# A decoder trunk on one core: the experts' sum starts at zero, and each expert's rows bring half of the residual

## The chip, the cores and the metric

One core of a Trainium2 chip. The metric is device time in microseconds (us) of one execution. The engines are TensorE (PE; PEld is its weight load), VectorE (DVE), ScalarE (ACT), GpSimd (POOL) and SyncE (SP). Each has its own queue and takes its instructions in order; they meet through semaphores. Transfers are started from SP, ACT or POOL.

## The reference, cut to what matters

Two layers. Each is attention (three kinds of heads and one output projection), a sum with the scaled input and a layer norm, then a mixture of experts and a second layer norm. Each of the 512 tokens goes to one group of four, and to two of the eight experts in that group:

```
for l in range(DEPTH):                                   # 2
    mix = hybrid_mixer(x, ...)
    x = layer_norm(ALPHA * x + mix, ln1_g[l], ln1_b[l])
    moe = hier_moe(x, ...)      # top-1 group, top-2 experts, 32 experts of width 256
    x = layer_norm(ALPHA * x + moe, ln2_g[l], ln2_b[l])
```

So the second norm's input is, up to the factor ALPHA, the row x of the token plus two expert rows. x is a normalized row times the gain ln1_g plus the bias ln1_b.

## The kernel before

Everything is float32, with 1024 columns. Tokens lie in four tiles `yn[0..3]` of 128 rows. After the output projection each tile is normalized on ACT (L919), without gain and bias, and its rows are written to DRAM as `xd` from ACT's queue (L920). DVE works out the router's logits `Lg` (L917), the group maximum `gm` (L932), the chosen experts' mask `selb` (L960), the position of each token in its expert's list `posm` (L972), and one-hot matrices `oneh` (L1054). With these and a token table (`tok`) PE makes the lists: for each slot of an expert the index of its row (`ri`) and its weight (`rv`). An expert has 64 slots, and two experts make a pair of 128 rows.

`first_rows(i)` (L885 to L890) belongs to this stage: two DVE operations of 128x1024 multiply tile i by the gain and add the bias (both broadcast in `gb1`, loaded once a layer), and ACT's queue writes the result to the DRAM tensor `y2`. It is called for tiles 0 to 2 in the loop over tiles and for tile 3 after the first gathers. DVE's order mixes these operations into the routing. `y2` is the sum to which the experts' rows are added.

The expert stage runs over 16 pairs p, in these steps:

- gather (L1000, POOL): 128 rows of `xd` into one of two x slots of the tile `xroom`;
- turned (L1011 on PE, L1015 on ACT, L1017 on DVE): transposes, with gain and bias on the way out of PSUM, into `xg`;
- experts_up (L97, tile S): gate and up matmuls of both experts; experts_mid: silu on ACT (L1031) and the product `h` on DVE (L1032);
- experts_down: transposes of h (L297) copied to `hT`, then the matmuls into the two PSUM banks `o`; their evacuation, times the weight `rv`, by ACT (L1044, first 512 columns) and DVE (L1045, second 512) into one of three y slots of `xroom`, which take turns (`row_room`);
- scatter (L1046, POOL): an indirect transfer that adds the 128 rows to `y2`.

PE works in the order S(p), hT(p), o(p), S(p+1), with the transposes of later pairs in between. The weights, 6 MB a pair, come over SP's queue (L530) in units of 1.5 MB into a ring of 13 units; a unit is loaded again when its last reader is done. The x slots, the y slots and one of these units share `xroom`, and fill it. After the 16 pairs follow a short loop for experts with more than 64 tokens (overflow, 64 rows at a time), the reading of `y2` (L1251), and the second norm with `gb2`.

Of the kernel before, what the change touches and what calls it, by code (L numbers as in the profile page):

```python
# [64 lines left out]
def trunk(tc, a, out, dbg=None):  # L65
# [4 lines left out]
    with es:  # L70
# [177 lines left out]
        for l in range(DEPTH):  # L248
# [285 lines left out]


            dp = xhp.tile([128, 2 * NK * S], F32, name="dp", tag="xh")
            stC = small.tile([128, 3, NT, 2, 4], F32, name="stC", tag="stC", bufs=1)
# [344 lines left out]
            gb1 = norm_rows(0)  # L882
            y2 = dr.tile([S, D], F32, name="y2", tag="y2")

            def first_rows(i):  # L885

                z = yn[i] if i < NT - 1 else at.tile([128, D], F32, name="x1", tag="u", bufs=3)
                V.tensor_tensor(z, yn[i], gb1[:, 0], OP.mult)
                V.tensor_tensor(z, z, gb1[:, 1], OP.add)
                A.dma_start(y2[128 * i:128 * i + 128, :], z)  # L890

            load_next(2)
# [10 lines left out]
            for i in range(NT):  # L903
                z = yn[i]
                out_proj(i, 2, 768, 1024)
                if i == 0:
                    zt(NT - 1, 0, 3)
                    zt(NT - 1, 3, 6)
                zt(i, 6, 8)
                V.bn_stats(bst[i][:, 1], z[:, 512:1024])  # L910
                t = bank("S")
                for k in range(NK):
                    mm(t[:, :36], zT[i][:, k], rwg[:, k], k == 0, k == NK - 1)
                mv = norm_scale(bst[i], LN_EPS)
                lt = small.tile([128, 36], F32, name="lt", tag="lt")
                V.scalar_tensor_tensor(lt, rsum, mv[:, 0:1], t[:, :36], op0=OP.mult, op1=OP.subtract)
                V.scalar_tensor_tensor(Lg[:, i], lt, mv[:, 3:4], rb, op0=OP.mult, op1=OP.add)  # L917
                V.tensor_tensor(mv[:, 4:5], mv[:, 0:1], mv[:, 3:4], OP.mult)
                A.activation(z, z, AF.Identity, scale=mv[:, 2:3], bias=mv[:, 4:5])  # L919
                A.dma_start(xd[128 * i:128 * i + 128, :], z)  # L920
                if i:
                    first_rows(i - 1)
            xroom = xhp.tile([128, 2 * NK * S], F32, name="xroom", tag="xh")
# [80 lines left out]
            def turned(xr):  # L1004
# [13 lines left out]
                return xg  # L1018

            halves_ = ((0, 64), (64, 128))  # L1020

# [12 lines left out]

            def experts_down(h, w, rows):
                hT = cp.tile([128, 2, 128], F32, name="hT", tag="rw")
                transposes(hT.rearrange("p a b -> p (a b)"), [h[:, 0:128], h[:, 128:256]], 128)
                o = [bank("o") for _ in range(2)]
                for f in range(2):
                    for n in range(2):  # L1040
                        for j, (c0, c1) in enumerate(halves_):
                            last_on["PE"] = mm(o[n][c0:c1], hT[:, f, c0:c1], down(w[j], f, n), f == 0, f == 1)
                y = row_room()
                last_on["A"] = A.activation(y[:, 0:512], o[0], AF.Copy, scale=rows[1])  # L1044
                last_on["V"] = V.tensor_scalar(y[:, 512:1024], o[1], rows[1], None, op0=OP.mult)  # L1045
                return G.indirect_dma_start(out=y2, out_offset=bass.IndirectOffsetOnAxis(ap=rows[0], axis=0), in_=y,  # L1046
                                            in_offset=None, bounds_check=S - 1, oob_is_err=False, compute_op=OP.add)

            RI, XR, XG = {}, {}, {}

# [46 lines left out]
            for p in range(2):  # L1097
                fetch(p)
            first_rows(NT - 1)
            attn.__exit__(None, None, None)  # L1100
            moe = tc.tile_pool(name=f"moe{l}", bufs=1, reuse_waits="tile")
            mo = units["m"] = moe.__enter__()
            load_next(3)
            XG[0] = turned(XR.pop(0))
            lists(1)
# [30 lines left out]
            def overflow():  # L1136

                n_items = nc.values_load(eidi[0:1, MAX_ITEMS:MAX_ITEMS + 1], min_val=0, max_val=MAX_ITEMS)
                with tc.For_i(0, n_items) as item:
# [63 lines left out]
                    for f in range(2):  # L1203
                        for h, c in enumerate(two):
                            mm(o[c], hT[:, f], down(w, f, h), f == 0, f == 1)
                    y = row_room()
                    A.activation(y[0:64, 0:512], o[0:64], AF.Copy, scale=wr[0:64])
                    V.tensor_scalar(y[0:64, 512:1024], o[64:128], wr[64:128], None, op0=OP.mult)
                    G.indirect_dma_start(out=y2, out_offset=bass.IndirectOffsetOnAxis(ap=ri[0:64], axis=0), in_=y[0:64], in_offset=None,
                                         bounds_check=S - 1, oob_is_err=False, compute_op=OP.add)  # L1210

            for p in range(NE // 2):
# [4 lines left out]
                if p + 1 < NE // 2:  # L1217
                    XG[p + 1] = turned(XR.pop(p + 1))
                    fetch(p + 3)
                if p % 2 == 0 and p // 2 + 2 < NE // 4:  # L1220
                    lists(p // 2 + 2)
                st = experts_down(h, w, RI.pop(p))
                load_next()
# [3 lines left out]
                if p == 3:  # L1227
                    pieces()
                    gb2 = norm_rows(1)

            last = l == DEPTH - 1
            with tc.issue_after(last_on["PE"].ins), tc.issue_after(last_on["A"].ins), tc.issue_after(last_on["V"].ins), tc.issue_after(st.ins):
                if not last:
# [11 lines left out]
            for j in range(2):  # L1245
                yu = carve(unit("A", "yt"), 0, [2, D])
                for i in range(2):
# [7 lines left out]
            for i in range(NT):  # L1255
# [6 lines left out]
                for t, c in zip(src, halves):  # L1262
                    V.scalar_tensor_tensor(z[:, c], t, mv[:, 0:1], gb2[:, 0, c], op0=OP.subtract, op1=OP.mult)
                for c in halves if i in (0, 3) else [slice(0, 1024)]:
                    V.scalar_tensor_tensor(z[:, c], z[:, c], mv[:, 2:3], gb2[:, 1, c], op0=OP.mult, op1=OP.add)  # L1265
                if last:
# [76 lines left out]
```

## Time and profile before

| | us |
|---|---|
| median of 3 runs | 1382.35 (1379.83 to 1384.95) |
| the profiled execution | 1385.0 |
| its span in the trace | 1383.2 |
| expert stage, first to last scatter, layer 0 | 434.98 to 660.88 |
| expert stage, first to last scatter, layer 1 | 1108.26 to 1330.18 |

The page is of one execution. Its first part gives each engine's busy time, its second the busy share in 40 slices of 34.6 us, with the granted TensorE clock and the share of the DMA engines. The views of the trace give the instructions of a stretch in order of time, each with the idle time of its engine before it and what ended that, and for transfers the time from issue to landing. A time of a row is from the start of the span.

### The profile page before, as it was taken

The numbers are of one execution on the slowest core, as the hardware profiler recorded it, in microseconds if no ns is written. First come the engines' busy times: TensorE is split into PE (matmuls) and PEld (weight loads), VectorE is DVE, ScalarE is ACT, GpSimd is POOL, SyncE is SP. The second block draws the span as 40 slices with busy tenths as digits, with TensorE's granted clock in tenths as the row PEclk, the third lists the DMA queues.
The fourth block names the chain that finished last, engine by engine and source line by source line (L and its number), as shares of the span: only waits on it lengthen the run. The fifth ranks groups of instructions, "written<-read, shape, count | busy, mean of one in ns | idle before, by whom it ended". The sixth has DMA issues, their size and how long they took to land. (4 is left out here: it accounts for less than half of the span.)

```text
span 1383.2 us, 18273 instructions
## 1 busy us (share of the span) xinstructions
PE 1194.4 (86%) x6701; PEld 815.8 (59%) x6708; DVE 696.6 (50%) x1822; ACT 442.9 (32%) x1050; POOL 292.5 (21%) x286
## 2 busy tenths in 40 slices
PE   6989999999939989887599999999996699898860
PEld 6989976668924533222398899666795343332320
DVE  7599638684552422111668892668636333211125
ACT  3362256673102221111235322857611122111100
POOL 5332431201001121100332334230000122111011
PEclk9999999999969999999799999999998799999985
DMA  7321440115397999998552224200426899999943
GB/s 240 116 80 51 128 158 11 36 40 185 118 402 279 400 413 405 409 390 287 166 165 78 65 83 140 98 23 22 156 104 247 347 384 407 409 403 410 356 166 123
DMA packets 63898, 293.81 MB, mean 212 GB/s; under 512 B 16064, under 2 KB 20672, under 8 KB 48192
## 3 DMA queue, kind: packets, MB, share of 16 engines
q1 hardware_dynamic: 52128, 267.43, 50.5%
q0 software_dynamic: 9376, 16.81, 4.9%
q10 hardware_dynamic: 2304, 8.39, 1.5%
q8 instruction: 54, 0.88, 0.3%
q14 instruction: 36, 0.29, 0.1%
HBM read 278.06 MB, written 31.82 MB: 224 GB/s over the span
## 5 line engine op out<-in xcount | busy, mean ns | idle before, releaser
L97 PE MATMUL acc<-U,xh 128*128 128x384 f32 (+1 forms) x1584 | 298.9, 343 | 18.9 <-DVE xh L212 7.0
L97 PEld LDWEIGHTS acc<-U,xh 128*128 128x128 f32 x1584 | 280.5, 193 | 21.9 <-issue 6.9
L97 PE MATMUL S<-w,xg 128*64 128x512 f32 (+1 forms) x968 | 272.0, 608 | 10.6 <-DMA w<-w_e 8.9
L97 PEld LDWEIGHTS S<-w,xg 128*64 128x64 f32 x968 | 83.1, 141 | 138.8 <-issue 112.9
L1017 DVE TENSOR_SCALAR xg<-acc,lv 128x128 f32<-128x128 f32 x128 | 45.8, 404 | 179.6 <-PE S L97 142.9
L97 PE MATMUL o<-w,hT 128*64 128x512 f32 x488 | 125.4, 603 | 5.9 <-ACT hT L90 3.4
L199 POOL TENSOR_TENSOR U<-raw,U 128x768 fp32r<-128x768 f32 (+2 forms) x46 | 90.3, 1967 | 166.9 <-ACT U L196 166.9
L1046 POOL DMA_INDIRECT y<-xroom,ri x32 | 51.4, 1607 | 294.8 <-DVE xroom L1045 180.5
L1031 ACT ACTIVATE h<-S 128x256 f32<-128x256 f32 x32 | 12.3, 383 | 270.6 <-PE S L97 270.6
L196 ACT ACTIVATE U<-raw 128x768 fp32r<-128x768 f32 (+2 forms) x88 | 68.0, 812 | 71.6 <-PE acc L97 43.7
L1045 DVE TENSOR_SCALAR xroom<-o,rv 128x512 f32<-128x512 f32 x32 | 24.0, 751 | 117.7 <-PE o L97 117.7
L97 PEld LDWEIGHTS o<-w,hT 128*64 128x64 f32 x488 | 39.2, 138 | 67.1 <-issue 57.4
L1000 POOL DMA_INDIRECT xroom<-xd,ri x33 | 35.2, 1066 | 180.5 <-PE acc L1011 94.5
L199 DVE TENSOR_TENSOR U<-raw,U 128x768 fp32r<-128x768 f32 (+2 forms) x42 | 52.8, 1260 | 36.5 <-ACT U L196 34.0
L1011 PEld LDWEIGHTS acc<-cst,xroom 128*128 128x128 f32 x256 | 29.4, 147 | 60.6 <-issue 36.0
L90 ACT ACTIVATE uc<-T 128x512 f32<-128x512 f32 (+3 forms) x117 | 51.3, 460 | 40.9 <-PE T L297 39.1
L1015 ACT ACTIVATE xg<-acc,lv 128x128 f32<-128x128 f32 x128 | 48.9, 458 | 45.5 <-PE T L97 35.8
L1011 PE MATMUL acc<-cst,xroom 128*128 128x128 f32 x256 | 43.7, 298 | 22.7 <-DMA xroom<-xd,ri 20.7
L97 PE MATMUL acc<-U,oh 128*128 128x384 f32 (+1 forms) x384 | 63.3, 315 | 0.0
L1044 ACT ACTIVATE xroom<-o,rv 128x512 f32<-128x512 f32 x32 | 22.0, 687 | 111.0 <-PE o L97 111.0
L97 PEld LDWEIGHTS acc<-U,oh 128*128 128x128 f32 x384 | 56.8, 189 | 1.2 <-issue 1.0
L403 DVE MATCH_REPLACE8 uc<-m,uc 128x256 f32<-128x256 f32 (+2 forms) x96 | 51.4, 539 | 0.0
(367 smaller groups left out, 1942.0 us busy)
## 6 DMA issues: line engine op xcount, KB each, us to landing
w<-w_e SPq DMA_DIRECT2D x110, 1536.0 KB
raw<-w_in SPq DMA_DIRECT2D x64, 384.0 KB
xroom<-w_e SPq DMA_DIRECT2D x8, 1536.0 KB
w<-w_e SPq DMA_DIRECT2D x24, 512.0 KB
raw<-w_o SPq DMA_DIRECT2D x16, 384.0 KB
gb<-ln_rows SPq DMA_DIRECT2D x4, 1024.0 KB
xd<-yn ACTq DMA_DIRECT2D x8, 512.0 KB
y<-yn ACTq DMA_DIRECT2D x6, 512.0 KB
```

Of the source, the lines that this page charges most:

```text
L90: A.activation(o, i, AF.Copy, scale=1.0 if scale is None else scale)
L97: return PE.matmul(o, l, r, start=start, stop=stop, skip_group_check=True)
L196: A.activation(hi, r, AF.Copy)
L199: e.tensor_tensor(lo, r, hi.bitcast(F32), OP.subtract)
L403: V.match_replace(out=acc_t[i][:, :n], in_to_replace=m8, in_values=acc_t[i][:, :n], imm_value=TAKEN)
L1000: G.indirect_dma_start(out=xr[0:n], out_offset=None, in_=xd, in_offset=bass.IndirectOffsetOnAxis(ap=ri[0:n], axis=0), bounds_check=S - 1, ...
L1011: PE.transpose(t[:, 128 * j:128 * j + 128], xr[:, 128 * k:128 * k + 128], ident)
L1015: A.activation(xg[:, k], o, AF.Identity, scale=lv[:, 0, k, 0:1], bias=lv[:, 0, k, 1:2])
L1017: V.tensor_scalar(xg[:, k], o, lv[:, 0, k, 0:1], lv[:, 0, k, 1:2], op0=OP.mult, op1=OP.add)
L1044: last_on["A"] = A.activation(y[:, 0:512], o[0], AF.Copy, scale=rows[1])
L1045: last_on["V"] = V.tensor_scalar(y[:, 512:1024], o[1], rows[1], None, op0=OP.mult)
L1046: return G.indirect_dma_start(out=y2, out_offset=bass.IndirectOffsetOnAxis(ap=rows[0], axis=0), in_=y, in_offset=None, bounds_check=S - 1, ...
```

## The change

- `y2` is made in the attention stage: POOL fills a small tile with zeros and one transfer on SP's queue writes it over all of `y2` (2 MB). `first_rows` is gone, with its eight DVE pairs and its eight transfers.
- `gb1` is multiplied by 0.5 on ACT, once a layer.
- A new function `half_rows` (L1016 to L1021 of the changed kernel) takes the next y slot and writes half of the gathered rows, times gain plus bias, into it: two DVE operations of 128x1024 (L1019, L1020). It is called one pair ahead, beside `turned`. Since each token has two expert rows, the two halves add up to its residual row.
- The two evacuations from PSUM become two DVE operations that add `o` times the weight to the y slot (L1048). ACT has none of it any more. The scatter (now L1049) is as it was. The overflow loop does the same with 64 rows.
- The second norm's gain and bias come in two transfers on SP's queue after the expert weights, into parts of the units that also hold the rows of `y2`.

```diff
@@ attention
+            y2 = dr.tile([S, D], F32, name="y2", tag="y2")
+            none = ring("P")
+            G.memset(none, 0.0)
+            SP.dma_start(y2.rearrange("(p r) c -> p (r c)", r=NT).rearrange("p (n c) -> p n c", c=512), none.unsqueeze(1).to_broadcast([128, 2 * NT, 512]))
@@ out_proj and routing
             gb1 = norm_rows(0)
-            y2 = dr.tile([S, D], F32, name="y2", tag="y2")
-
-            def first_rows(i):
-
-                z = yn[i] if i < NT - 1 else at.tile([128, D], F32, name="x1", tag="u", bufs=3)
-                V.tensor_tensor(z, yn[i], gb1[:, 0], OP.mult)
-                V.tensor_tensor(z, z, gb1[:, 1], OP.add)
-                A.dma_start(y2[128 * i:128 * i + 128, :], z)
-
+            A.activation(gb1.rearrange("p a d -> p (a d)"), gb1.rearrange("p a d -> p (a d)"), AF.Copy, scale=0.5)
...
-                if i:
-                    first_rows(i - 1)
...
+            def half_rows(xr, n=128):
+
+                y = row_room()
+                V.tensor_tensor(y[0:n], xr[0:n], gb1[0:n, 0], OP.mult)
+                V.tensor_tensor(y[0:n], y[0:n], gb1[0:n, 1], OP.add)
+                return y
+
@@ experts_down
-            def experts_down(h, w, rows):
+            def experts_down(h, w, rows, y):
...
-                y = row_room()
-                last_on["A"] = A.activation(y[:, 0:512], o[0], AF.Copy, scale=rows[1])
-                last_on["V"] = V.tensor_scalar(y[:, 512:1024], o[1], rows[1], None, op0=OP.mult)
+                for n in range(2):
+                    c = slice(512 * n, 512 * n + 512)
+                    last_on["V"] = V.scalar_tensor_tensor(y[:, c], o[n], rows[1], y[:, c], op0=OP.mult, op1=OP.add)
@@ the loop over pairs
-                    XG[p + 1] = turned(XR.pop(p + 1))
+                    XG[p + 1], HR[p + 1] = turned(XR[p + 1]), half_rows(XR.pop(p + 1))
                     fetch(p + 3)
...
-                st = experts_down(h, w, RI.pop(p))
+                st = experts_down(h, w, RI.pop(p), HR.pop(p))
...
-                    gb2 = norm_rows(1)
...
+            yus = [unit("A", "yt") for _ in range(2)]
+            gb2 = [yu[:, 2 * D:3 * D] for yu in yus]
+            for j in range(2):
+                SP.dma_start(gb2[j], a["ln_rows"][l:l + 1, 1, j].to_broadcast([128, D]))
```

A scheduler sets the order within each engine, so the order of the program text is not the order of the queues. First DVE's queue in the expert stage of layer 1, around the evacuation of pair 6 (PE_49, Activation_49, DVE_49 and DMASW0 to DMASW7 are semaphores: of engines, and of POOL's indirect transfers, which take the eight in turn). The kernel before, from the copy of hT(6) to the xg of pair 9:

```order
L92 COPY hT<-T 128x256 [waits PE_49]
L1017 TENSOR_SCALAR xg<-acc,lv 128x128
L1045 TENSOR_SCALAR xroom<-o,rv 128x512 [waits PE_49]
L1017 TENSOR_SCALAR xg<-acc,lv 128x128 [waits PE_49]
L1032 TENSOR_TENSOR h<-h,S 128x256 [waits Activation_49]
L1017 TENSOR_SCALAR xg<-acc,lv 128x128 x3
```

The same place in the changed kernel, from the copy of hT(6) to the xg of pair 9:

```order
L92 COPY hT<-T 128x256 [waits PE_49]
L1013 TENSOR_SCALAR xg<-acc,lv 128x128
L1048 SCALAR_TENSOR_TENSOR xroom<-o,rv,xroom 128x512 [waits PE_49] x2
L1019 TENSOR_TENSOR xroom<-xroom,gb 128x1024 [waits DMASW3_49,DMASW0_49,DVE_49]
L1020 TENSOR_TENSOR xroom<-xroom,gb 128x1024 [waits DVE_49]
L1013 TENSOR_SCALAR xg<-acc,lv 128x128 [waits PE_49]
L1035 TENSOR_TENSOR h<-h,S 128x256 [waits Activation_49]
L1013 TENSOR_SCALAR xg<-acc,lv 128x128 x3
```

Between the rows of y(6) and the product h(7) now stand the half rows of pair 9, and the first of them waits for two indirect transfers: the gather of pair 9, whose rows it reads, and the scatter of pair 6, whose slot it takes.

The second place is DVE's queue in the routing of layer 1, from the mask of the chosen experts to the one-hots. The kernel before:

```order
L955 MATCH_REPLACE hot<-top_8922,le 128x8 x3
L888 TENSOR_TENSOR x_9040<-yn,gb 128x1024 [waits Activation_49]
L956 TENSOR_SCALAR hot<-hot 128x32 [waits DVE_49]
L889 TENSOR_TENSOR x_9040<-x_9040,gb 128x1024 [waits DVE_49]
L960 TENSOR_TENSOR selb<-ghot,hot 128x128 [waits DVE_49]
L972 SCALAR_TENSOR_TENSOR posm<-S,selb 128x128 [waits DVE_49,PE_49]
L888 TENSOR_TENSOR yn<-yn,gb 128x1024 [waits DMAHW1_49]
L1054 TENSOR_TENSOR oneh<-posm,cst 128x256 [waits DVE_49]
L889 TENSOR_TENSOR yn<-yn,gb 128x1024 [waits DVE_49]
L1054 TENSOR_TENSOR oneh<-posm,cst 128x256 x3
```

The changed kernel, the same stretch:

```order
L951 MATCH_REPLACE hot<-top_8940,le 128x8 x3
L952 TENSOR_SCALAR hot<-hot 128x32 [waits DVE_49]
L956 TENSOR_TENSOR selb<-ghot,hot 128x128 [waits DVE_49]
L968 SCALAR_TENSOR_TENSOR posm<-S,selb 128x128 [waits DVE_49,PE_49]
L1114 COPY cnt<-S 128x32
L1057 TENSOR_TENSOR oneh<-posm,cst 128x256 [waits DVE_49]
L1057 TENSOR_TENSOR oneh<-posm,cst 128x256 x3
```

The four operations of first_rows are gone from between the mask and the one-hots, and with them the wait for DMAHW1, the write of a tile's rows to `xd`.

## Rows read from the trace of the kernel before

**Rows 1.** The page: busy time of the engines, and the DMA share by slices.

```profile
PE 1194.4 (86%) x6701; PEld 815.8 (59%) x6708; DVE 696.6 (50%) x1822; ACT 442.9 (32%) x1050; POOL 292.5 (21%) x286
...
DMA  7321440115397999998552224200426899999943
```

**Rows 2.** The chain that ended last: start us, us, what; first and last piece.

```profile
1205.24 35.27 DMA w<-w_e
...
1303.25 13.78 DMA w<-w_e
```

**Rows 3.** Stretches: length, busy of PE, PEld, DVE, ACT, POOL, clock, DMA, GB/s.

```profile
1180.00:1240.00 60.00, 53.43 (x244) 19.49 (x242) 14.74 (x50) 10.63 (x26) 10.50 (x8) 1.00 1.02 408
```

**Rows 4.** DVE in time, routing of layer 1: start us, us, instruction, [idle before <-releaser].

```profile
1055.92 0.17 DVE L932 TENSOR_REDUCE gm<-Lg 128x4 f32<-128x16 f32 x1
...
1061.25 0.28 DVE L960 TENSOR_TENSOR selb<-ghot,hot 128x128 bf16<-128x128 f32 x1
1062.14 0.29 DVE L972 SCALAR_TENSOR_TENSOR posm<-S,selb 128x128 f32<-128x128 f32 x1 [0.60 <-PE S L97]
1067.73 1.22 DVE L888 TENSOR_TENSOR yn<-yn,gb 128x1024 f32<-128x1024 f32 x1 [5.30 <-DMA xd<-yn]
...
1070.35 1.09 DVE L1054 TENSOR_TENSOR oneh<-posm,cst 128x256 fp32r<-128x256 f32 x3
```

**Rows 5.** DVE in time, the same place in layer 0.

```profile
382.76 0.17 DVE L932 TENSOR_REDUCE gm<-Lg 128x4 f32<-128x16 f32 x1
387.66 1.23 DVE L888 TENSOR_TENSOR yn<-yn,gb 128x1024 f32<-128x1024 f32 x1 [4.74 <-DMA xd<-yn]
...
395.03 0.29 DVE L960 TENSOR_TENSOR selb<-ghot,hot 128x128 bf16<-128x128 f32 x1
```

**Rows 6.** The chain that ended last: the first gather of layer 1.

```profile
1077.57 10.06 DMA xroom<-xd,ri
```

**Rows 7.** POOL in time: the first and sixteenth scatter of each layer.

```profile
434.98 1.63 POOL L1046 DMA_INDIRECT y<-xroom,ri  x1 [7.17 <-issue]
...
660.88 2.13 POOL L1046 DMA_INDIRECT y<-xroom,ri  x1 [15.48 <-ACT U L196]
...
1108.26 1.62 POOL L1046 DMA_INDIRECT y<-xroom,ri  x1 [7.47 <-issue]
...
1330.18 1.63 POOL L1046 DMA_INDIRECT y<-xroom,ri  x1 [13.68 <-DVE h L1146]
```

**Rows 8.** All engines in time: one pair of layer 1, from xg to the next scatters.

```profile
1295.49 0.41 DVE L1017 TENSOR_SCALAR xg<-acc,lv 128x128 f32<-128x128 f32 x1 [8.08 <-PE S L97]
...
1295.91 0.42 DVE L1032 TENSOR_TENSOR h<-h,S 128x256 f32<-128x256 f32 x1
...
1296.38 0.44 PE L297 MATMUL T<-cst,h 128*128 128x128 f32 x2 [0.94 <-DVE h L1032]
...
1301.00 0.75 DVE L1045 TENSOR_SCALAR xroom<-o,rv 128x512 f32<-128x512 f32 x1 [3.71 <-PE o L97]
...
1302.48 1.56 POOL L1046 DMA_INDIRECT y<-xroom,ri  x1 [12.72 <-issue]
...
1314.94 1.55 POOL L1046 DMA_INDIRECT y<-xroom,ri  x1 [10.90 <-DVE xroom L1045]
```

**Rows 9.** The scatter's line L1046: issue to landing, all 32.

```profile
DMA to landing us min/median/max: 6.8/10.5/12.0
```

**Rows 10.** A stretch after a gap of PE, columns as in rows 3.

```profile
590.00:592.00 2.00, 1.21 (x5) 0.79 (x5) 1.79 (x6) 1.40 (x5) 0.00 (x0) 0.50 1.01 424
```

**Rows 11.** All engines in time, around that stretch.

```profile
586.68 0.64 PE L97 MATMUL S<-xroom,xg 128*64 128x512 f32 x1 [1.95 <-DMA xroom<-w_e]
...
590.61 0.66 PE L297 MATMUL T<-cst,h 128*128 128x128 f32 x2 [1.02 <-DVE h L1032]
...
597.01 0.75 DVE L1045 TENSOR_SCALAR xroom<-o,rv 128x512 f32<-128x512 f32 x1 [4.96 <-PE o L97]
```

**Rows 12.** The scatter's line L1046 again, the one at 1302.48 alone.

```profile
DMA to landing us min/median/max: 9.1/9.1/9.1
```

More of the change, by code (lines that the diff above doesn't have):

```diff
@@ L1042, in experts_down @@
                             last_on["PE"] = mm(o[n][c0:c1], hT[:, f, c0:c1], down(w[j], f, n), f == 0, f == 1)
-                y = row_room()
-                last_on["A"] = A.activation(y[:, 0:512], o[0], AF.Copy, scale=rows[1])
-                last_on["V"] = V.tensor_scalar(y[:, 512:1024], o[1], rows[1], None, op0=OP.mult)
+                for n in range(2):
+                    c = slice(512 * n, 512 * n + 512)
+                    last_on["V"] = V.scalar_tensor_tensor(y[:, c], o[n], rows[1], y[:, c], op0=OP.mult, op1=OP.add)
                 return G.indirect_dma_start(out=y2, out_offset=bass.IndirectOffsetOnAxis(ap=rows[0], axis=0), in_=y,
                                             in_offset=None, bounds_check=S - 1, oob_is_err=False, compute_op=OP.add)
-            RI, XR, XG = {}, {}, {}
+            RI, XR, XG, HR = {}, {}, {}, {}
             def hots(b):
@@ L1098, in trunk @@
                 fetch(p)
-            first_rows(NT - 1)
             attn.__exit__(None, None, None)
@@ L1103, in trunk @@
             load_next(3)
-            XG[0] = turned(XR.pop(0))
+            XG[0], HR[0] = turned(XR[0]), half_rows(XR.pop(0))
             lists(1)
@@ L1205, in overflow @@
                             mm(o[c], hT[:, f], down(w, f, h), f == 0, f == 1)
-                    y = row_room()
-                    A.activation(y[0:64, 0:512], o[0:64], AF.Copy, scale=wr[0:64])
-                    V.tensor_scalar(y[0:64, 512:1024], o[64:128], wr[64:128], None, op0=OP.mult)
+                    y = half_rows(xr, 64)
+                    V.scalar_tensor_tensor(y[0:64, 0:512], o[0:64], wr[0:64], y[0:64, 0:512], op0=OP.mult, op1=OP.add)
+                    V.scalar_tensor_tensor(y[0:64, 512:1024], o[64:128], wr[64:128], y[0:64, 512:1024], op0=OP.mult, op1=OP.add)
                     G.indirect_dma_start(out=y2, out_offset=bass.IndirectOffsetOnAxis(ap=ri[0:64], axis=0), in_=y[0:64], in_offset=None,
@@ L1228, in trunk @@
                     pieces()
-                    gb2 = norm_rows(1)
             last = l == DEPTH - 1
-            with tc.issue_after(last_on["PE"].ins), tc.issue_after(last_on["A"].ins), tc.issue_after(last_on["V"].ins), tc.issue_after(st.ins):
+            yus = [unit("A", "yt") for _ in range(2)]
+            gb2 = [yu[:, 2 * D:3 * D] for yu in yus]
+            for j in range(2):
+                SP.dma_start(gb2[j], a["ln_rows"][l:l + 1, 1, j].to_broadcast([128, D]))
+            with tc.issue_after(last_on["PE"].ins), tc.issue_after(last_on["V"].ins), tc.issue_after(st.ins):
                 if not last:
@@ L1245, in trunk @@
             for j in range(2):
-                yu = carve(unit("A", "yt"), 0, [2, D])
+                yu = carve(yus[j], 0, [2, D])
                 for i in range(2):
@@ L1262, in trunk @@
                 for t, c in zip(src, halves):
-                    V.scalar_tensor_tensor(z[:, c], t, mv[:, 0:1], gb2[:, 0, c], op0=OP.subtract, op1=OP.mult)
+                    V.scalar_tensor_tensor(z[:, c], t, mv[:, 0:1], gb2[0][:, c], op0=OP.subtract, op1=OP.mult)
                 for c in halves if i in (0, 3) else [slice(0, 1024)]:
-                    V.scalar_tensor_tensor(z[:, c], z[:, c], mv[:, 2:3], gb2[:, 1, c], op0=OP.mult, op1=OP.add)
+                    V.scalar_tensor_tensor(z[:, c], z[:, c], mv[:, 2:3], gb2[1][:, c], op0=OP.mult, op1=OP.add)
                 if last:
```

## The prediction

> **What bounds the kernel now.** I read the page first. TensorE (PE) is busy 86% of the span and VectorE (DVE) 50%, and the DMA engines stand at nine tenths in three long stretches of the slices; in the third slice they are at two tenths [rows 1]. These shares are averages over unlike stages, so the stages come next. The chain of waits, followed back from the end, is made of weight transfers from 1205 to 1317 us, four pieces from 35.27 to 13.78 us [rows 2]. The table by stretches says the same of the middle of the expert stage: DMA share 1.02 at 408 GB/s, PE 53.43 of 60 us, DVE only 14.74 [rows 3]. A pair's weights are 6 MB, and at this rate they take some 15 us. So the expert stage lasts as long as its weights, and DVE has slack. Ahead of it lies a stage of another kind, the routing: a serial chain of small DVE operations, then index lists, a gather, and the first transposes of the expert stage [rows 4 to 6]. A microsecond off that chain starts the expert stage a microsecond earlier.
>
> The scatters give the pitch of the pairs: the first of layer 0 starts at 434.98 and the sixteenth at 660.88, 225.9 us or 15.1 a pair; in layer 1 from 1108.26 to 1330.18, 221.9 us or 14.8 [rows 7].
>
> **What goes: first_rows.** Each call is two DVE operations of 128x1024 of 1.22 us and a 512 KB transfer. In layer 1 two of them stand between gm and selb: 1055.92 to 1061.25 is 5.33 us, of which 2.4 go. From posm at 1062.14 the one-hots' last three start at 1070.35, 8.21 us later; of this only posm itself (0.29) and one one-hot (1.09 for three, 0.36) are needed. The rest, 7.6, is the L888 that waited 5.30 us for the write of xd, and the pair of operations itself [rows 4]. One more operation stands ahead of the last Lg, 1.2. Sum: 11.2 us. In layer 0 the way from gm at 382.76 to selb at 395.03 is 12.27 us, with a wait of 4.74 on the same write inside [rows 5]; without guests it takes layer 1's 5.33 less 2.4, so 2.9. Gain 9.3. What is late next is the gather, issued at 1077.57, 10.06 us to landing, and only then come the first transposes [rows 6]. It starts from the lists and moves with them, unless xd itself is late; the writes of xd leave ScalarE's queue now without the y writes between them, so I expect the whole 20.5 us. Bounds: 10 (the gather then waits for xd) to 24.
>
> **What is added off the path.** Zeroing y2 is a small memset and 2 MB written in the third slice's quiet [rows 1], some 5 us of transfer at the 408 GB/s of [rows 3], all covered; 0 to 1, and 5 if that cover were gone. Scaling gb1 is one ScalarE operation a layer over 2048 columns, early in attention where the engine has gaps; 0 to 2.4 by twice the 1.22 us of DVE's 1024 columns. Loading gb2 moves from the early stage to the end of the expert weights, 1 MB, 2.5 us at the same rate, beside the overflow loop; 0 to 2.5, and I take 1 for all of these. Each layer starts with three half_rows, 7.3 us of DVE, between the first transposed rows and the first h; they lie under the first pair's matmuls in part. I take 2 us a layer, with bounds 0 and 7.
>
> **What is added on the path: a wait in the middle of DVE's queue.** half_rows is two operations of 1.22 us, 2.4 a pair, and the two additions from PSUM replace one evacuation of 0.75 on DVE and one on ScalarE [rows 8]. By busy time that is harmless: about 3.2 us a pair more on an engine that is busy a quarter of the stage. But half_rows writes a y slot, there are three, and it writes one pair ahead. So the half rows of pair p+3 go into the slot that the scatter of pair p is still reading. In the new order they stand directly behind the additions of pair p, as the excerpt from DVE's order shows, and wait there for a scatter that has only just been issued. Before, the slot was written again by an evacuation three pairs later, some 45 us on. Queued behind the wait on DVE are the xg of pair p+3 and the product h of pair p+1; behind h are the transposes hT and the matmuls o of p+1 on PE, behind these the additions of p+1, and behind these the next scatter. That is a closed chain, once around for each pair, for thirteen half_rows a layer (pairs 3 to 15).
>
> One round, at full clock: landing of the scatter 10.5 us, the median of all 32 [rows 9]; wake-up 0.1; half_rows 2.4; the first xg 0.42 (1295.49 to 1295.91); h to the transposes 0.47 (to 1296.38); from there to the end of o 4.62 (the last evacuation starts at 1301.00); one addition 0.75, as that evacuation, since the first addition's bank is ready earlier; and 0.73 to the scatter's start at 1302.48 [rows 8]. Sum 20.0 us, against 14.8 to 15.1 that the weights need.
>
> The clock adds to this. After o(p) PE has the next S (some 8 us) and then nothing until hT, 5 to 6 us. After a much shorter gap, 1.95 us before 586.68, the granted clock stood at half (0.50, the 1.2 GHz level) between 590 and 592 [rows 10, 11], and there the same piece, transposes to end of o, went from 590.61 to 597.01: 6.40 us instead of 4.62 [rows 11]. I take this 1.8 for every round: 21.8 us.
>
> A layer then has one pitch of 15.8 (scatter 0 to 1: landing, half_rows, small operations, two additions, issue: 10.5 + 0.1 + 2.4 + 0.6 + 1.5 + 0.7), twelve of 21.8, which is 261.6, and two free ones of 12.46 (1302.48 to 1314.94 [rows 8]): 302.3 us from the first scatter to the sixteenth. Against 225.9 and 221.9 the layers lose 76.4 and 80.4.
>
> The landing is the term that decides. All 32 of this trace lie between 6.8 and 12.0 [rows 9], and the one at 1302.48, when the weight queue was running out, took 9.1 [rows 12]. In the new rhythm the transfers wait for slots and are not always there, which speaks for 9 to 10; freed slots are refilled just when the scatter starts, which speaks for 10 to 11. I take the median and keep 9.1 and 12.0 as ends: minus 36 and plus 39 us over 26 rounds.
>
> The Trainium skill speaks against a long landing: "DMA: Bandwidth & Descriptors", section "Anatomy of one DMA — SWDGE (gpsimd) path", gives a transfer issued from GpSimd about 2.0 us and its bytes at 436 GB/s. For this scatter's 512 KB that would be 3.2 us, an estimate from that page. The trace differs: no scatter here lands under 6.8 us, and the measurement decides.
>
> **Sum against the profiled run.** 1385.0 - 20.5 + 4 + 1 + 76.4 + 80.4 = 1526.3 us. That run lies 2.65 us above the median of the three, so by the median 1524 us.
>
> **Rivals.**
> (A) The same wait, but the clock stays at 2.4 GHz, because the gap before hT is filled or too short: 24 rounds less 1.8 us each, 43 us: 1481. For it speaks that the clock was 1.00 over the whole of 1180 to 1240 though PE had gaps there [rows 3]; against it that those gaps were shorter than the new ones.
> (B) The scatter is gone from the slot before the half rows want it, so the wait costs nothing and only the routing gain is left: 1385.0 - 20.5 + 5 - 2.65 = 1367, faster. A round without the landing is 9.5 us at full clock, so it decides at a landing of about 5.5 us, where the round fits under the weights' 15. By the page of the Trainium skill named above that would be so. Against it: the shortest of 32, 6.8 us, belongs to the last scatter of a layer, and even it would give a round of 16.3.
> (C) The wait as forecast, but the routing gain does not come, since the gather is held by the writes of xd, which DVE waited for until 1067.73 [rows 4]: 1524 + 20 = 1544. For it: these writes take that long in both layers [rows 4, 5]. Against: in those traces the queue carried the y writes among them, which are gone.
> (D) The half rows wait, but in part: the scheduler's order is fixed, yet landings of 7 to 8 us in a half-idle DMA give rounds of 17 to 18 with a full clock: some 1420 to 1440.
>
> **How the numbers follow.** Forecast 0.60, A 0.20, C 0.08, B 0.06, D 0.06. Predicted is the likeliest, 1524. The landing's ends and a clock that falls in some rounds only join the forecast with A; the range 1455 to 1568 leaves out B, most of D, A with short landings, and the longest landings together with C. B alone is faster; nothing lies within 0.5% (about what a measurement of this kernel can tell from no change) except a B that loses most of its routing gain. So faster 0.05, same 0.01, slower 0.94.
>
> **What will show it.** In the profile of the changed kernel: the first multiplication of half_rows (L1019) waiting on the transfer y<-xroom,ri, some 6 to 8 us each, 26 times; scatters 20 to 22 us apart instead of 15, with two short pitches at the end of a layer; PE idle 5 to 6 us a round with its granted clock down behind it; the DMA share of the stage down from 1.0 to about 0.7; the first transposes of the expert stage some 10 us earlier in each layer. It is wrong if L1019 does not wait, or if the pitch stays at 15 although it does; then something else in the round has slack that I have not seen. If the transposes start no earlier, the routing part is wrong by itself.

## The result, and the profile after

The changed kernel takes 1528.39 us, median of four runs (1526.55 to 1531.72), against 1383.65 (1379.83 to 1386.05) before: 1.105 times as long, with a 95% interval of 1.102 to 1.109. The forecast was 1524, slower.

The page of the changed kernel, with its busy times, the granted clock and the DMA share in 40 slices of 38.2 us:

```profile
span 1526.6 us, 18261 instructions
PE 1229.8 (81%) x6708; PEld 827.4 (54%) x6708; DVE 780.5 (51%) x1905; ACT 424.7 (28%) x1019; POOL 298.1 (20%) x288
PEclk9999999999788888789799999999989787787886
DMA  7422420052897878674543243013378877876633
```

The long stretches in which the transfers stood at nine tenths [rows 1] are gone: one slice of 9 is left, the others of the expert stages (slices 12 to 20 and 31 to 39) show 6 to 8, and 3 to 5 at the ends, where the weights run out. Over most of the stage of layer 1 the DMA share is 0.76 and the granted clock 0.80, against 1.02 and 1.00 in [rows 3] (columns as there):

```profile
1182.00:1449.00 267.00, 179.47 (x704) 67.52 (x706) 85.25 (x198) 24.72 (x68) 33.67 (x24) 0.80 0.76 290
```

Work has grown by less than the time (DVE by 83.9 us, PE by 35.4, ScalarE has 18.2 less), and no engine's share of the span has risen by more than a point, so most of the time is waiting. Which wait, the line of half_rows tells (its instructions, then what ended its idle time in us and times):

```profile
L1019 DVE TENSOR_TENSOR xroom<-xroom,gb x33: 1217/1226/1227, 403.8 to 1482.3; 128x1024 f32<-128x1024 f32 x32, 64x1024 f32<-64x1024 f32 x1
  DMA y<-xroom,ri: 262.8, 26
  DMA xroom<-xd,ri: 18.6, 5
```

26 waits for a scatter, 13 a layer, 10.1 us each. The scatters, first and second, fourteenth and sixteenth of each layer (POOL in time), answer to [rows 7]:

```profile
423.89 1.63 POOL L1049 DMA_INDIRECT y<-xroom,ri  x1 [7.52 <-DVE xroom L1048]
439.19 1.59 POOL L1049 DMA_INDIRECT y<-xroom,ri  x1 [9.78 <-DVE xroom L1048]
...
704.60 1.55 POOL L1049 DMA_INDIRECT y<-xroom,ri  x1 [18.75 <-DVE xroom L1048]
...
730.08 1.90 POOL L1049 DMA_INDIRECT y<-xroom,ri  x1 [11.52 <-DVE xroom L1048]
...
1165.47 1.62 POOL L1049 DMA_INDIRECT y<-xroom,ri  x1 [8.38 <-DVE xroom L1048]
1182.10 1.59 POOL L1049 DMA_INDIRECT y<-xroom,ri  x1 [11.97 <-DVE xroom L1048]
...
1448.57 1.56 POOL L1049 DMA_INDIRECT y<-xroom,ri  x1 [19.07 <-DVE xroom L1048]
...
1474.06 1.59 POOL L1049 DMA_INDIRECT y<-xroom,ri  x1 [11.53 <-DVE h L1148]
```

From the second to the fourteenth they are 265.4 and 266.5 us apart, 22.1 and 22.2 a pair. The difference of the spans, 143.4 us, is the sum of a few pieces. Layer 0 reaches its first scatter 11.1 us earlier and then takes 306.2 in place of 225.9; layer 1 comes from layer 0's last scatter to its own first in 435.4 in place of 447.4, 12.0 less, and takes 308.6 in place of 221.9. That is -11.1 + 80.3 - 12.0 + 86.7, and 0.5 less behind the last scatter.

One round of layer 1, all engines in time, from one scatter to the next (it answers to [rows 8]):

```profile
1318.99 1.59 POOL L1049 DMA_INDIRECT y<-xroom,ri  x1 [7.69 <-DVE xroom L1048]
...
1326.95 0.59 PE L97 MATMUL S<-w,xg 128*64 128x512 f32 x1
...
1329.48 1.23 DVE L1019 TENSOR_TENSOR xroom<-xroom,gb 128x1024 f32<-128x1024 f32 x1 [8.18 <-DMA y<-xroom,ri]
1330.74 1.23 DVE L1020 TENSOR_TENSOR xroom<-xroom,gb 128x1024 f32<-128x1024 f32 x1
...
1332.00 0.41 DVE L1013 TENSOR_SCALAR xg<-acc,lv 128x128 f32<-128x128 f32 x1
1332.33 0.41 DVE L1035 TENSOR_TENSOR h<-h,S 128x256 f32<-128x256 f32 x1
...
1332.89 0.66 PE L297 MATMUL T<-cst,h 128*128 128x128 f32 x2 [5.35 <-DVE h L1035]
...
1338.17 1.64 DVE L1048 SCALAR_TENSOR_TENSOR xroom<-o,rv,xroom 128x512 f32<-128x512 f32 x2 [3.84 <-PE o L97]
...
1340.09 1.58 POOL L1049 DMA_INDIRECT y<-xroom,ri  x1 [7.20 <-DVE xroom L1048]
```

Read it downwards: PE is done with S at 1327.5, and ACT with silu soon after; h needs 0.41 us of DVE. But DVE stands at half_rows until the scatter of 1318.99 has landed, 10.5 us after its issue, then works 2.5 us on rows that are needed two pairs later, and only then does h. PE waits 5.35 us for it. In the whole kernel this wait of PE grew from 20.1 us to 163.6 (first the kernel before, in us, times and longest; then the changed one, where the last two numbers are PE's idle time before this line and the part that ended with h):

```profile
PE T L297 <- DVE h L1032: 20.1, 21, 1.0
```

```profile
L297 PE MATMUL T<-cst,h 128*128 128x128 f32 x64 | 19.6, 404 | 163.6 <-DVE h L1035 163.6
```

PE's clock in the round above, around that gap (columns as in [rows 3]):

```profile
1328.00:1330.00 2.00, 0.00 (x0) 0.00 (x0) 0.52 (x1) 1.36 (x4) 0.00 (x0) 0.94 1.04 436
1330.00:1332.00 2.00, 0.00 (x0) 0.00 (x0) 1.94 (x2) 0.00 (x0) 0.55 (x1) 0.50 0.94 399
1332.00:1334.00 2.00, 1.11 (x5) 0.93 (x5) 1.79 (x6) 0.00 (x0) 0.89 (x1) 0.50 1.07 455
1334.00:1336.00 2.00, 2.00 (x7) 0.65 (x8) 0.33 (x2) 0.00 (x0) 0.00 (x0) 0.50 0.90 377
1336.00:1338.00 2.00, 2.00 (x12) 0.59 (x10) 0.00 (x0) 0.00 (x0) 0.00 (x0) 0.85 0.24 94
1338.00:1340.00 2.00, 2.00 (x10) 0.61 (x7) 1.50 (x2) 0.00 (x0) 0.00 (x0) 1.00 0.21 37
```

The clock is at its lower level (0.50, 1.2 GHz) while the o matmuls start (1334.1 us), and the transfers run dry at the end of the round (0.21): SP's queue starts no load of weights between 1325.8 and 1339.0, since it waits until PE is done with a unit.

### The profile page after: what moved, and what is told of

It is laid out like the page before. It is cut to its first block, busy times and chain, and to the rows that moved or that the text cites. A ratio compares the mean times of both kernels' runs of the same rounds, so it can differ in the third digit from the quotient of the medians.

```text
span 1526.6 us, 18261 instructions
## 1 busy us (share of the span) xinstructions
PE 1229.8 (81%) x6708; PEld 827.4 (54%) x6708; DVE 780.5 (51%) x1905; ACT 424.7 (28%) x1019; POOL 298.1 (20%) x288
## 5 line engine op out<-in xcount | busy, mean ns | idle before, releaser
L97 PE MATMUL acc<-U,xh 128*128 128x384 f32 (+1 forms) x1584 | 298.7, 343 | 17.6 <-DVE xh L212 7.2
L97 PEld LDWEIGHTS acc<-U,xh 128*128 128x128 f32 x1584 | 280.9, 194 | 20.2 <-issue 7.2
L97 PE MATMUL S<-w,xg 128*64 128x512 f32 (+1 forms) x968 | 270.2, 610 | 2.5 <-DVE xg L1191 2.5
L1019 DVE TENSOR_TENSOR xroom<-xroom,gb 128x1024 f32<-128x1024 f32 (+1 forms) x33 | 40.4, 1225 | 281.4 <-DMA y<-xroom,ri 262.8
L97 PE MATMUL o<-w,hT 128*64 128x512 f32 x488 | 162.0, 751 | 5.3 <-ACT hT L90 3.4
L97 PEld LDWEIGHTS S<-w,xg 128*64 128x64 f32 x968 | 83.7, 142 | 129.7 <-issue 118.9
L297 PE MATMUL T<-cst,h 128*128 128x128 f32 x64 | 19.6, 404 | 163.6 <-DVE h L1035 163.6
L1034 ACT ACTIVATE h<-S 128x256 f32<-128x256 f32 x32 | 12.3, 384 | 440.3 <-PE S L97 440.3
L1049 POOL DMA_INDIRECT y<-xroom,ri x32 | 51.1, 1598 | 368.9 <-DVE xroom L1048 340.7
L1048 DVE SCALAR_TENSOR_TENSOR xroom<-o,rv,xroom 128x512 f32<-128x512 f32 x64 | 47.7, 750 | 122.4 <-PE o L97 118.9
L297 PEld LDWEIGHTS T<-cst,h 128*128 128x128 f32 x64 | 8.7, 189 | 183.8 <-issue 95.9
L97 PEld LDWEIGHTS o<-w,hT 128*64 128x64 f32 x488 | 46.7, 174 | 92.8 <-issue 80.7
L196 ACT ACTIVATE U<-raw 128x768 fp32r<-128x768 f32 (+2 forms) x88 | 68.1, 812 | 83.9 <-PE acc L97 42.0
L996 POOL DMA_INDIRECT xroom<-xd,ri x33 | 40.1, 1215 | 250.0 <-issue 146.1
L97 PE MATMUL acc<-U,oh 128*128 128x384 f32 (+1 forms) x384 | 63.3, 315 | 0.0
L1007 PE MATMUL acc<-cst,xroom 128*128 128x128 f32 x256 | 45.5, 311 | 21.2 <-DMA xroom<-xd,ri 13.3
L97 PEld LDWEIGHTS acc<-U,oh 128*128 128x128 f32 x384 | 56.8, 189 | 1.2 <-issue 1.0
## 6 DMA issues: line engine op xcount, KB each, us to landing
xroom<-w_e SPq DMA_DIRECT2D x4, 768.0 KB, 10.7
```

The source lines that it names most:

```text
L97: return PE.matmul(o, l, r, start=start, stop=stop, skip_group_check=True)
L196: A.activation(hi, r, AF.Copy)
L297: PE.transpose(t[:rows, 128 * j:128 * j + 128], b, ident)
L996: G.indirect_dma_start(out=xr[0:n], out_offset=None, in_=xd, in_offset=bass.IndirectOffsetOnAxis(ap=ri[0:n], axis=0), bounds_check=S - 1, ...
L1007: PE.transpose(t[:, 128 * j:128 * j + 128], xr[:, 128 * k:128 * k + 128], ident)
L1019: V.tensor_tensor(y[0:n], xr[0:n], gb1[0:n, 0], OP.mult)
```

## The experiments

**e1: the half rows behind h.** If the wait in front of h is the cause, holding the half rows behind it must bring the pitch back.

```diff
-                    XG[p + 1], HR[p + 1] = turned(XR[p + 1]), half_rows(XR.pop(p + 1))
+                    XG[p + 1] = turned(XR[p + 1])
+                    with tc.issue_after(last_on["h"].ins):      # h of pair p
+                        HR[p + 1] = half_rows(XR.pop(p + 1))
...
```

(`issue_after` holds an instruction behind another one in the queue; `last_on["h"]` is the product h. The line that sets it is left out here and below.)

> The changed kernel with one thing moved: the half rows of pair p+1 are held behind the product h of pair p in DVE's queue (they stood up to one and a half pairs further ahead). The same operations, the same three y slots. Theory (the wait for the scatter in the middle of DVE's queue makes the round): by then the scatter of pair p-2 was issued some 22 us before, so no half row waits, the pitch falls to the weights' 15 us, and what is left is the routing gain: 1362 to 1375 us, faster than before. Rival (the added DVE operations, 3.2 us a pair on the way from one scatter to the next, make it slow by themselves): about 1383 - 20 + 32 x 3.2 = 1465. Risk of its own: the x slot comes free later, and the gather that follows may be late for the transposes by 1 to 3 us a pair.

Measured: 1440.12 us, 1.038 times before (1.033 to 1.043). No half row waits for a scatter any more, and still the pitch rises at the sixth scatter: the next four are 21.6 to 24.2 us apart in layer 0 and 23.2 to 24.1 in layer 1, those behind them, up to the fourteenth scatter, 16 to 25. That is a miss, and not the rival's way either: e5 below does the same DVE work in 1362. One round tells why (all engines in time):

```profile
1206.17 1.64 POOL L996 DMA_INDIRECT xroom<-xd,ri  x1 [17.20 <-issue]
...
1215.98 0.87 PE L1007 MATMUL acc<-cst,xroom 128*128 128x128 f32 x3 [6.50 <-DMA xroom<-xd,ri]
1216.78 7.34 PE L97 MATMUL S<-w,xg 128*64 128x512 f32 x22
...
1228.29 0.42 DVE L1035 TENSOR_TENSOR h<-h,S 128x256 f32<-128x256 f32 x1
1228.63 1.22 DVE L1019 TENSOR_TENSOR xroom<-xroom,gb 128x1024 f32<-128x1024 f32 x1
...
1230.08 1.22 DVE L1020 TENSOR_TENSOR xroom<-xroom,gb 128x1024 f32<-128x1024 f32 x1
...
1230.88 1.33 POOL L996 DMA_INDIRECT xroom<-xd,ri  x1 [18.71 <-issue]
```

half_rows is also a reader of the gathered rows. Behind h it frees its x slot late; the next gather takes that slot, lands 9.7 us later, and in PE's order its transposes stand ahead of S, which h needs. Gather, transposes, S, h, half rows: 24.7 us, a second closed chain in place of the first. PE waits 93.8 us for gathered rows in this kernel, 13.3 in the changed one. I had named this risk and priced it at 1 to 3 us a pair.

**e2: the half rows one pair further ahead, behind the h before.** Against e1:

```diff
-                    with tc.issue_after(last_on["h"].ins):      # h of pair p
+                    with tc.issue_after((hm1 if p else last_on["h"]).ins):      # hm1: h of pair p-1
```

> As the run before, but the half rows of pair p+1 are held behind the product h of pair p-1, one pair earlier. Then the scatter of pair p-2 was issued some 8 us before them; with a landing of 10.5 us they wait 2 to 3 us, but behind h, beside the matmuls o, which take 4.6. Theory: the wait is there and costs next to nothing: 1362 to 1380 us. If what counts is that DVE waits at all, and not what stands behind the wait: 24 rounds some 3 to 5 us longer, about 1450.

Measured: 1398.30, 1.011 (1.008 to 1.015). Waits of DVE and PE in this kernel (us in total, times, longest):

```profile
DVE xroom L1019 <- DMA y<-xroom,ri: 131.0, 23, 9.9
...
PE T L297 <- DVE h L1035: 42.8, 28, 4.6
...
PE acc L1007 <- DMA xroom<-xd,ri: 40.1, 9, 8.2
```

The same kind of wait, 23 times and 5.7 us each, costs 36 us more than none (1362, below) where the change's 262.8 us of waiting cost 166. The wait is longer than the 2 to 3 us I had expected, and the time is between my two cases. Two waits of PE are left of it, about equal: against e5, PE waits 21.0 us more for h (21.8 there) and 21.3 more for gathered rows (18.8 there). So part of this loss is again the x slot, which comes free late when its reader stands waiting for a scatter.

**e3: four y slots, the order left to the scheduler.**

```diff
             def row_room():
                 turns["y"] += 1
-                return carve(xroom, UNIT + 2 * D + D * (turns["y"] % 3), [D])
+                if turns["y"] % 4 == 3:
+                    return mo.tile([128, D], F32, name="y4", tag="y4")
+                return carve(xroom, UNIT + 2 * D + D * (turns["y"] % 4), [D])
```

> The changed kernel with a fourth y slot. The order is made anew, and moves the half rows further ahead: from pair 9 on in each layer the half rows of pair p+4 stand directly behind the additions of pair p, ahead of h of pair p+1, again in the slot that the scatter of pair p is reading; for pairs 4 to 8 they stand behind h. Theory (place in the queue decides): seven rounds a layer stay at 22 us, the others come down to 15 to 17: 1460 to 1490 us. Rival (the number of slots decides): no wait, about 1365.

Measured: 1497.1 in one run. What ended the idle time before its half rows (us, times; `y` is the fourth slot):

```profile
  DMA xroom<-xd,ri: 116.9, 18
  DMA y<-xroom,ri: 99.6, 10
  DMA y<-y,ri: 49.1, 4
```

14 waits for a scatter are left, seven a layer, 10.6 us each. The pitch is 22.7 in layer 0 from the fifth scatter to the thirteenth, and 14.6, 12.4 and 13.1 after that. That is 7 us above the 1460 to 1490 expected, and the first line shows where more was lost: the earlier half rows, which now stand further ahead, wait for their own gathers, and from the first scatter of layer 0 to its fifth it takes 70.5 us in place of 50.0 in the kernel before. One more slot moved the same wait to a later pair, since the scheduler filled the new distance as well. Room alone gave back 31 of the 166 us that e5, below, gives back.

**e4: the routing part alone.**

```diff
-                    XG[p + 1], HR[p + 1] = turned(XR[p + 1]), half_rows(XR.pop(p + 1))
+                    XG[p + 1] = turned(XR.pop(p + 1))
...
-                    last_on["V"] = V.scalar_tensor_tensor(y[:, c], o[n], rows[1], y[:, c], op0=OP.mult, op1=OP.add)
+                y = row_room()
+                last_on["A"] = A.activation(y[:, 0:512], o[0], AF.Copy, scale=rows[1])
+                last_on["V"] = V.tensor_scalar(y[:, 512:1024], o[1], rows[1], None, op0=OP.mult)
```

> The routing part alone. y2 starts at zero and first_rows is gone, but half_rows is left out as well and the two evacuations are those of the kernel before, on ScalarE and DVE: the residual row is missing from the sum. Theory: only the gain ahead of the expert stage is left, some 20 us over two layers: 1355 to 1370 us. If the gather or the writes of xd take the place of the wait: 1375 to 1383.

Measured: 1341.94, 0.970 (0.968 to 0.973), 13 us below the range. Without the residual the second layer's routing is another, and the overflow loop at the end is not there (behind the last scatter the kernel is 20.3 us shorter); up to the sixteenth scatter of layer 1, 1306.82 against 1330.18 [rows 7], it is 23.4 us ahead. The two expert stages take 226.2 and 221.4 us, as before. So the gain lies ahead of the expert stages, and is some 23 us: 9.0 in layer 0 (first scatter at 425.97) and 14.1 between the layers.

**e5: e2 and e3 together.** Order and room; the edit is those of e2 and e3.

> The order of e2 (half rows of pair p+1 behind the product h of pair p-1) and a fourth y slot, so that the slot was last read by the scatter of pair p-3, two pairs ago. Nothing is left to wait for: neither the scatter, since it has long landed, nor the gather, whose x slot comes free some 3 us later than before. Theory (two conditions: the wait must stand behind h, and the slot must be free): pitch 15 us, 1362 to 1375 us, faster than before by about the routing gain of 20 us. If the DVE work itself costs (3.2 us a pair): the 1398 of e2 stays, or falls by 5 at most.

Measured: 1362.47, 0.986 (0.984 to 0.988): faster than both. Neither of the two edits does this alone. The half rows wait for no scatter (the line's only idle time is four waits for gathers, 18.2 us), and the stretch of layer 1 in the middle of the expert stage reads:

```profile
1105.00:1290.00 185.00, 164.34 (x720) 59.89 (x718) 79.23 (x186) 23.80 (x66) 32.94 (x22) 0.98 1.00 394
```

The DMA share is 1.00 again, the clock 0.98. DVE is busy 79.23 of 185 us, against 14.74 of 60 in [rows 3], so it does all of the added work, and the expert stages take 224.7 and 221.6 us, no more than before. The DVE work by itself costs no time that the runs show.

**e6: e1 and a third x slot.** It cuts e1's chain at the other end.

```diff
-                xr = carve(xroom, UNIT + D * (turns["x"] % 2), [D])
+                xr = mo.tile([128, D], F32, name="x3", tag="x3") if turns["x"] % 3 == 2 else carve(xroom, UNIT + D * (turns["x"] % 3), [D])
```

> The order of e1 (half rows of pair p+1 behind h of pair p, three y slots, no wait for a scatter) and a third x slot, so that a gather no longer needs the slot that the half rows have just read. In e1 the half rows, the gather into their slot (9.6 us), the transposes ahead of S and S itself formed a closed chain of 24 us. If that is why e1 was slow, the chain is gone here and the pitch is 15 us: 1362 to 1375 us. If e1 was slow for another reason (DVE work in the way of the transposed rows xg), it stays near 1440.

Measured: 1361.52, 0.984 (0.982 to 0.986), 79 us less than e1 by one buffer. The reading of e1 is right.

**e7: the kernel before, with first_rows later.** Is it enough to take first_rows out of the routing chain, without any of the rest?

```diff
-                if i:
-                    first_rows(i - 1)
...
-            first_rows(NT - 1)
+            with tc.issue_after(last_on["ri"].ins):     # behind the first lists
+                for i in range(NT):
+                    first_rows(i)
```

> The kernel before with one thing moved: all four first_rows are held on DVE behind the index lists of the first batch. Nothing of the change is in it: no zeros, no half rows, and the expert stage is that of before. If the routing gain comes from DVE's queue (the operations and their wait for the write of xd), it comes here as well: 1360 to 1368 us, and the expert stage loses nothing. If it needs the four writes of y2 out of the way (they share ScalarE's queue with xd): 1375 to 1383. Risk: the tiles that first_rows reads lie where the first weights of the ring go, so these may start later; 0 to 5 us a layer.

Measured: 1383.65, 1.0005 (0.9992 to 1.0018): nothing, where 1360 to 1368 was expected. The routing did get faster: the first gather stands at 393.53 in layer 0 and at 1063.42 in layer 1, in the kernel before at 403.73 and, [rows 6], at 1077.57. It is lost behind that: the first scatter is 7.9 us earlier than before in layer 0 and 0.9 in layer 1, the sixteenth 3.4 and 0.2. The issue on POOL in layer 1 and SP's queue in layer 0 (POOL in time, SP in time):

```profile
1063.42 9.80 POOL L998 DMA_INDIRECT xroom<-xd,ri  x1 [13.78 <-DVE ri L984]
1073.52 1.02 POOL L998 DMA_INDIRECT xroom<-xd,ri  x1 [0.31 <-issue]
```

```profile
402.27 0.33 SPq L243 DMA_DIRECT2D gb<-ln_rows  x1
402.65 14.13 SPq L530 DMA_DIRECT2D w<-w_e  x6
```

In layer 1 the gather's issue took 9.80 us and its landing 18.9, in the very stretch in which DVE runs the eight operations of first_rows. In layer 0 SP's queue stands at the next load of `gb`, which must wait until first_rows has read it, and the weights behind it start at 402.65; in the kernel before they start at 393.08. That these two take the gain is read from the traces; e10 and e11 take up the second of them.

**e9: half the scatter.**

```diff
-                return G.indirect_dma_start(out=y2, out_offset=bass.IndirectOffsetOnAxis(ap=rows[0], axis=0), in_=y,
+                return G.indirect_dma_start(out=y2, out_offset=bass.IndirectOffsetOnAxis(ap=rows[0][0:64], axis=0), in_=y[0:64],
...
```

> The changed kernel with a scatter of the first 64 rows of each pair only, 256 KB in place of 512; the second expert's rows of each pair are left out of the sum. The order on DVE, the three slots and the place of the wait are the same. Theory (a round is the landing of the scatter plus 11.6 us for all the rest): the pitch of the pairs 1 to 13 falls by just as much as the landing does, so with a landing of 7 to 9 us it is 18.5 to 20.5 in place of 22.1. Rival (the round is made by something else on DVE or PE): the landing falls and the pitch stays at 22. The second layer's routing changes with the values, so the overflow loop may be gone; only the pitches are read.

Measured: 1618.15 in one run, with six rounds of the overflow loop at the end in place of one, since the routing changed; only the pitch counts. Landing of the scatters of layer 0 between 430 and 700 us, first in this kernel, then in the changed one:

```profile
DMA to landing us min/median/max: 4.6/7.9/8.6
```

```profile
DMA to landing us min/median/max: 9.2/10.6/11.7
```

The landing falls by 2.7 us, and the pitch from the second scatter to the fourteenth from 22.1 to 19.4 (437.93 to 671.15), also by 2.7. In layer 1 they fall by 2.8 (10.7 to 7.9) and 3.1 (22.2 to 19.1). A round is the landing and 11.2 to 11.5 us for the rest, close to one for one.

**e8: PE kept busy in its gap.**

```diff
+                if 3 <= p < 14:
+                    with tc.issue_after(last_on["S"].ins):      # the last matmul of S(p)
+                        warm(24)                                # 128x512 on constants
                 h = experts_mid(gu)
```

> The changed kernel with 24 matmuls on constants (128x512, bf16) put behind S of the pairs 3 to 13, where PE waits for hT; they fill some 5 of the 6 to 7 us that it idles there. The wait for the scatter is untouched. Theory (1.8 us of each round is the half clock after the idle time): 22 rounds less 1.5 to 1.8 us each, 35 to 40 us: about 1490. If the clock term is an accident of single rounds: 1520 to 1535. If the extra matmuls are themselves in the way: above 1535.

Measured: 1539.57 in one run, the third of my cases: the added matmuls are in the way. For the sum it is inconclusive. The o matmuls did get faster, 633 ns the mean one against 751 in the changed kernel and 603 before, but the added matmuls went ahead of the transposes of the next pair, and PE then waited for those rows (L97 of this kernel: busy, mean ns, idle before it):

```profile
L97 PE MATMUL S<-w,xg 128*64 128x512 f32 x936 | 284.1, 642 | 30.4 <-DVE xg L1013 30.4
```

So the clock's part is seen in the matmuls (21.8 us of busy time less on the o group), and not as time won.

**e10 and e11: the loading of gb2.** e11 is that part of the change alone, on the kernel before; e10 is e7 with it.

```diff
-                    gb2 = norm_rows(1)
...
+            yus = [unit("A", "yt") for _ in range(2)]
+            gb2 = [yu[:, 2 * D:3 * D] for yu in yus]
+            for j in range(2):
+                SP.dma_start(gb2[j], a["ln_rows"][l:l + 1, 1, j].to_broadcast([128, D]))
```

> As e7 (the kernel before with all first_rows behind the lists), and gb2 loaded as in the changed kernel, after the expert weights, so that SP's queue no longer waits in front of the weights until first_rows has read gb1. In e7 the stream of weights started again at 402.65 and 1071.60, as late as or later than before. If that took e7's gain in layer 0, some 8 to 10 us come back there. In layer 1 the first gather of e7 was on POOL for 9.8 us while DVE ran the eight operations of first_rows; that stays, so little is won there. Sum: 1366 to 1376 us. If only the y2 writes beside the gathers were the trouble: 1380 to 1385, as e7.

> One part of the change alone: the kernel before with gb2 loaded after the expert weights, in two transfers into parts of the yt units; first_rows and all else as before. SP's queue no longer waits for first_rows. My prediction gave this part 0 to 2.5 us of loss, taking 1. If the weights that bound the expert stage start earlier by it, there is a gain of up to some 10 us a layer: 1363 to 1378. If the start is set by DVE's routing chain alone: 1380 to 1386.

Measured: e11 1385.24, 1.0001 (0.9987 to 1.0014), nothing; the prediction had up to 2.5 us of loss for this part. e10 1378.08, 0.995 (0.993 to 0.997), a third of e5's gain and 2 us outside the 1366 to 1376 expected. In its profiled run, the slowest of the four at 1382.36, the sixteenth scatter is 1.7 us earlier than before in layer 0 and 3.0 in layer 1. So the 8 to 10 us that I expected in layer 0 did not come: there the load that stands in SP's way is now that of the next layer's gb1, at 403.38, with the weights again behind it. In layer 1 the first gather again sits on POOL, for 9.70 us. In the changed kernel there is neither: gb1 is read until the end of the expert stage, so SP's queue has no load of `gb` in front of the weights, and DVE has no first_rows beside the first gathers. That these two together make the difference between e7 and e4 is argued from the traces; no run took away both and kept first_rows.

## Why the prediction was right, point by point

- **What bounds the kernel**: the weights before, the round after. e5 brings back the DMA share of 1.00 and with it the old length of the stages; so does e6, with 222.9 and 219.7 us.
- **The closed chain**: as forecast, 13 half rows a layer, each waiting for the scatter that has just been issued. e9 shows that the landing goes into the pitch one for one, e5 that without the wait nothing of the loss is left. e2, e3 and e5 together show that it takes both the place in the queue and the reuse of a slot.
- **Size of a round**: forecast 21.8, measured 22.1 and 22.2. The landing taken was 10.5; the median of all is 10.5 again, and 10.6 in the middle of layer 0. The rest is 11.5 in place of 11.3. The layers take 306.2 and 308.6 in place of 302.3.
- **The clock**: forecast 1.8 us a round from two rows. In the changed kernel the o matmuls take 751 ns in place of 603, 36.6 us more busy time in all (162.0 against 125.4), 1.4 a round; the transposes of h before them add 5.4 in all (19.6 against 14.2), 0.2 a round. Another measure: from these transposes to the first addition a waiting round takes 5.2 to 8.0 us, other work of PE in between included; behind the scatter of 1448.57, with nothing to wait for and the clock at 1.00, it takes 3.83. Rival A, a full clock, is out: it would have given 20.0, and over the rounds of layer 1 the granted clock is 0.80. No run holds the wait and lifts the clock cleanly (e8), so the 1.8 is borne out in size, not tested by itself.
- **The routing gain**: forecast 20.5, less 4 for a later first scatter, 16.5 in all; measured 11.1 and 12.0, 23.1. The term that was furthest off is the 2 us a layer for the first three half rows: e4, which has none, gains the same 23.1. The other 2.6 are in the removed operations and waits themselves, though the way from gm to selb, 3.28 us in both layers, is a little longer than the 2.9 forecast for layer 0 [rows 5]. Rival C is out.
- **Rival B**, the landing too short to matter, is out; the scatters between the first and the thirteenth of a layer land in 8.6 to 12.3 us. So is the 3.2 us that I had worked out from the Trainium skill's page "DMA: Bandwidth & Descriptors", section "Anatomy of one DMA — SWDGE (gpsimd) path": the shortest scatter of this trace, the last of all, takes 4.8 us, and the shortest with half the bytes 4.3.
- **Rival D**, landings of 7 to 8 us at a full clock, is out by the same numbers.
- **A slip in what was to be seen**: I wrote waits of 6 to 8 us for L1019. They are 10.1. DVE is idle from the end of its additions, or of the small list operations behind them, and not from the moment at which h could start; what the wait costs is the shorter stretch, PE's 5.35 us in the round above.

The sum came within 3 us of the profiled run (1526.3 against 1528.5) by two errors of opposite sign, 6.6 us too little gain and 10.2 too little loss. That the sum is so close is luck; the chain, the number of its rounds and the length of a round, within 0.4 us, are not.

## What to carry to other kernels

When a tile is filled ahead of its use, ask what last read the slot, when that reader ends, and what stands behind the fill in its engine's queue: here 262.8 us of waiting on an engine that is half idle set the time of the kernel, since the product that feeds TensorE stood behind it. The scheduler here moved work ahead into the fourth slot too, so a new buffer and an order had to come together; with the order alone the kernel stayed 36 us (e2) and 78 us (e1) above e5, with the buffer alone (e3) 135. A step that reads a buffer and writes another holds both, and moving it away from one wait can close a chain through the other, as in e1; there a third x slot (e6) opened it.

## What the runs showed of the hardware

The issue of a gather on GpSimd took 9.80 us in e7 and 9.70 in e10, in layer 1, while DVE ran eight operations of 128x1024 from 1061.96 to 1071.2 us; elsewhere it takes 1.0 to 1.9. (In e10 the same eight ran from 1064.33 to 1073.6.) The Trainium skill, "SBUF — State Buffer", section "SBUF: two separate sides", says that GpSimd cannot write a transfer's descriptors while DVE runs an operation in a 2-port mode. By the same section of the Trainium skill, a DVE operation with two inputs in SBUF and a GpSimd operation that reads SBUF also exclude each other, and the one that starts second waits. The eight have two inputs there, a tile of rows and `gb1`, so this would fit layer 1, if issuing a gather, whose indices `ri` lie in SBUF, counts as such an operation. But in layer 0 of e7 and of e10 the same gather took 1.84 us beside the same operations. The cause stays open.
